# Feed-forward with seven block products: buffers for sums of weights, two products' weights made earlier, token sums in quarters

## The chip, the cores and the metric

The kernel runs on one core of a Trainium2 chip. The metric is the time on the device in microseconds (us) of one execution; the median of some runs is given. The five engines of the core are named as in the profile: PE (matmul; PEld is its weight load), DVE (VectorE), ACT (ScalarE), POOL (GpSimd) and SP (SyncE, which issues the transfers here).

## The reference, cut to what matters

The reference is two blocks of a transformer on 1024 tokens of width 1024. The change lies in the last part of the second block, the feed-forward with a gate: 5632 columns up (2816 of gate, 2816 of value), a causal convolution over three tokens for each column, and 2816 rows down.

```python
f = causal_dwconv(rms_norm_2(h, norm_ffn_pre[l]) @ ffn_up[l], ffn_conv[l])
gate, val = jnp.split(f, 2, axis=-1)
f = (jax.nn.gelu(gate, approximate=True) * val) @ ffn_down[l]
h = h + rms_norm_2(f, norm_ffn_post[l])
```

## The kernel before, in words

The program is written for a framework with tiles and pools: the author writes operations and buffers, and a scheduler sets the order of the instructions on each engine from its own costs. A tile with `bufs=n` under one tag turns through n buffers, and who writes a buffer again waits until its last reader is done.

Every fp32 operand of a matmul is held as two parts, high and low (`split`, lines 99 to 106: ACT rounds the high part, line 103, and DVE subtracts it, line 106). A product of two operands then takes three matmuls: high with high, high with low, low with high.

**Output projection** (`out_proj2`, to line 1617). It takes nine token tiles (t = -1 to 7). For each it multiplies by the output weights (128x512 matmuls, line 132 to 134), scales by the norm, adds the residual, writes the sum to HBM, norms again, transposes on PE (line 255) and leaves the columns in `hf` (line 1609). The two quadrants of `hf` that products use as they are go to `quads` as high and low parts (q0, q1).

**Up projection** (`ffn`, from line 1656). It runs 22 blocks j, and each makes 128 gate columns and 128 value columns of all tokens. Weights (two halves of the 1024 rows by gate and value columns) and tokens (two halves of the rows by two halves of the tokens) are each cut into 2x2 quadrants, and seven products instead of eight make the block (`SEVEN`): five of them take a sum or difference of two weight quadrants, and five take a sum or difference of two token quadrants.

- `up_raw` loads a block's weights as two transfers of 512 KB into `upraw` (two buffers).
- `up_op` makes the weights of product i in two pieces (128 x 2 x 128 each). Where a sum is wanted, POOL adds into `uptmp` (line 1648), ACT rounds it into `uph` and DVE makes `upl`. Before, `uptmp` has `bufs=1` in each of two pools, `w1` and `wp`, of which the pieces of line 1667 take `w1` nine times in eleven. The results `uph`, `upl` have two buffers in `wp` and nine in `w1`.
- `tok_op` makes the token sums s2 to s6 once, in block 0, and keeps them. Each sum is made in two slices of 4 x 258 or 4 x 256 columns: an add into the one buffer `tsum` (line 1682; POOL for i = 4 and 6, DVE for the rest), then a split.
- `block` runs the products. A product is two column ranges c of 12 matmuls of 128x258 each (lines 1700 to 1702), so a block is 7 x 2 x 12 = 168. ACT copies products 0 to 2 out of PSUM into `fs` (line 1706), DVE adds products 3 to 6 to them (`fx`, lines 1712 to 1720), POOL combines the `fs` (lines 1709, 1710, 1713, 1716), and `gate` makes the convolution and the gate: ACT (lines 1801, 1807), DVE (line 1803 eight times and line 1808 twice a block, both 128x512). Two transfers write `fd` to HBM (line 1809).

`ahead(t)` in `build` loads block 0's weights during the output projection and makes the weights of product 0.

**Down projection** (line 1780). It loads `fd` and the down weights and takes 22 steps for each half of the tokens; its first two steps are made ready during the up projection.

Of the kernel before, what the change touches and what calls it, by code (L numbers as in the profile page):

```python
# [13 lines left out]
F32 = mybir.dt.float32  # L14
F32R = mybir.dt.float32r
# [16 lines left out]
class Builder:  # L32
# [1601 lines left out]
            raws.append(raw)  # L1634
        return raws

    def up_op(self, raws, i, pools):

        nc = self.nc
        (r, h), sign, other = self.SEVEN[i][:3]  # L1640
        parts = []
        for raw in raws:
            pool, bufs = next(pools)
            src = raw[:, h, :, 128 * r:128 * r + 128]
            if sign:
                r2, h2 = other
                tmp = pool.tile([128, 2, 128], F32, tag="uptmp", name="uptmp", bufs=1)
                nc.gpsimd.tensor_tensor(tmp, src, raw[:, h2, :, 128 * r2:128 * r2 + 128],  # L1648
                                        op=ALU.add if sign > 0 else ALU.subtract)
                src = tmp  # L1650
            p = [pool.tile([128, 2, 128], F32R, tag="up" + z, name="up" + z, bufs=bufs) for z in "hl"]
            self.split(*p, src)
            parts.append(p)
        return lambda k: tuple(z[:, k % 2] for z in parts[k // 2])

    def ffn(self, hd, hf, close_hf, quads, wp, early, out):

        nc, I = self.nc, self.I
        st = ExitStack()
        sp = st.enter_context(self.pool("hS", 1))  # L1660
        w1 = st.enter_context(self.pool("wtsu", 1))
        p = st.enter_context(self.pool("ffn", 2))
# [1 line left out]
        nc.sync.dma_start(cw, I["ffn_conv"])  # L1664
        fd = [self.dp.tile([128, 2, 512], F32, name=f"fd{j}") for j in range(22)]
        self.psum(mm="ABDCABDE")
        pools = itertools.cycle([(wp, 2)] + [(w1, 9)] * 4 + [(wp, 2)] + [(w1, 9)] * 5)
        halves = [slice(0, 512), slice(512, 1024)]
        sums = {}

        def tok_op(i):

            qa, sign, qb = self.SEVEN[i][3:]
            if not sign:
                return quads[qa[0]]
            if i not in sums:
                a, b = (hf[:, 4 * r:4 * r + 4, 512 * h:512 * h + 514] for r, h in (qa, qb))
                op = [sp.tile([128, 4, 514], F32R, name=f"s{i}{z}") for z in "hl"]
                for c in (slice(0, 258), slice(258, 514)):
                    s = (slice(None), slice(None), c)  # L1680
                    t = sp.tile([128, 4, 258], F32, tag="tsum", name="tsum")[:, :, :c.stop - c.start]
                    (nc.gpsimd if i in (4, 6) else nc.vector).tensor_tensor(
                        t, a[s], b[s], op=ALU.add if sign > 0 else ALU.subtract)
                    self.split(op[0][s], op[1][s], t)
                sums[i] = op
            return sums[i]

        def block(j, raws, first):

            x = [[p.tile([128, 2, 258], F32, tag=f"fx{part}", name="fx") for part in range(2)] for c in range(2)]  # L1690
            s = [[None] * 7 for c in range(2)]
            for i in range(7):
                w = first if first and i == 0 else self.up_op(raws, i, pools)
                op = tok_op(i)
                for c in range(2):
                    ps = self.mm()[:, :258]
# [26 lines left out]
        raws, w0 = early  # L1723
# [17 lines left out]
        with ExitStack() as s2:  # L1741
            for j in range(22):
                if j:
                    raws, w0 = self.up_raw(j, wp), None
                block(j, raws, w0)
                if j == 0:
                    close_hf()
                    P = s2.enter_context(self.pool("dn1", 1, side="right"))
                if j == 20:
                    ready = [step(0, 0), step(0, 1)]  # L1750
# [60 lines left out]
    def build(self, out):  # L1811
# [77 lines left out]
        with ExitStack() as st:  # L1889
# [8 lines left out]
            def ahead(t):  # L1898
                if t == 3:
                    raws = self.up_raw(0, wp)  # L1900
                    early.extend((raws, self.up_op(raws, 0, itertools.repeat((wp, 2)))))

            self.out_proj2(wo2, oin2, o2, lod, hd, gp[:, 1], hf, quads, ahead)
            wos.close()
# [153 lines left out]
```

## Time and profile before

| | us |
|---|---|
| median of 3 runs | 3214.81 (3198.78 to 3215.32) |
| the profiled execution, its own time | 3207.53 |
| its span, first to last instruction | 3205.6 |
| PE busy over the span | 3034.4 (95%) |
| DVE, ACT, POOL busy | 1986.4 (62%), 1478.8 (46%), 786.2 (25%) |
| mean granted clock of TensorE | 0.972 |
| output projection 2 and first up products | about 2280 to 2404 |
| up projection, first matmul to last | 2391.2 to 2957.6 |
| down projection to the end | 2957.6 to 3205.6 |

Times in rows are counted from the start of the span. The median lies 7.3 us above the profiled execution's own time. The granted clock of a stretch is a share of full speed (2.4 GHz); 0.5 is the lower level, 1.2 GHz. Matmul durations overlap, so the distance between two starts is the time one takes of PE, and a stretch in which PE is "busy" throughout can still be slow at the lower clock.

### The profile page before, as it was taken

The page shows a single profiled execution, that of the slowest core. Times are in us where ns is not written, and L with a number is a line of the kernel's source. Part 1 is how long each engine was busy: PE and PEld are TensorE (multiplying, and loading weights), DVE is VectorE, ACT ScalarE, POOL GpSimd, SP SyncE. Part 2 cuts the span into 40 slices and gives each one's busy share as a digit, 9 for nine tenths or more (in the row PEclk, how much of TensorE's full clock was granted, in tenths as well). Part 3 has the DMA queues.
Part 4 walks back from the last instruction along what each step waited for, and adds up shares of the span by engine and source line. Part 5 has one row for each costly group of instructions (what it writes and reads, how often), then busy time and mean ns, then how long its engine had stood idle before and what let it go on. Part 6 is the DMA issues. An engine that isn't in the chain of part 4 may idle for free.

```text
span 3205.6 us, 54674 instructions
## 1 busy us (share of the span) xinstructions
PE 3034.4 (95%) x20419; PEld 2749.9 (86%) x20419; DVE 1986.4 (62%) x5238; ACT 1478.8 (46%) x3740; POOL 786.2 (25%) x892
## 2 busy tenths in 40 slices
PE   8899999999999999998999999999997999999999
PEld 5799999889877889997889898788877888888887
DVE  5667757777765755545457344766458677777453
ACT  4689845555653733332254222447434444444332
POOL 2466622332220000000000000110016565665000
PEclk9999999999999999999999999899997999999999
DMA  5222210010042221213311222313222122122552
GB/s 210 68 79 86 85 39 14 25 34 14 21 146 100 104 82 55 66 46 116 105 56 56 62 66 55 73 45 101 84 91 64 63 80 67 67 66 86 188 195 97
DMA packets 164137, 252.99 MB, mean 79 GB/s; under 512 B 25800, under 2 KB 93440, under 8 KB 163872
## 3 DMA queue, kind: packets, MB, share of 16 engines
q1 hardware_dynamic: 163872, 249.50, 24.3%
q8 instruction: 160, 2.62, 0.4%
q14 instruction: 105, 0.86, 0.1%
HBM read 194.94 MB, written 54.51 MB: 78 GB/s over the span
## 4 chain that ended last, share of the span: by engine, by line
PE 71%; DVE 12%; ACT 5%; POOL 5%; DMA 4%; issue 3%; SPq 0%; DVEq 0%; POOLq 0%; ACTq 0%
PE mm L132 12%; PE mm L133 12%; PE mm L134 12%; PE dn L1780 8%; DVE fy L1803 3%; PE te L405 3%; PE po L1534 3%; PE sc L391 3%; DVE upl L106 2%; PE po L661 2%; POOL uptmp L1648 2%; PE po L612 2%; PE mm L1702 1%; PE mm L1700 1%; PE mm L1701 1%
## 5 line engine op out<-in xcount | busy, mean ns | idle before, releaser
L132 PE MATMUL mm<-whi,hT 128*128 128x256 f32 (+1 forms) x1760 | 516.3, 294 | 17.5 <-DVE gs L428 4.7
L133 PE MATMUL mm<-wlo,hT 128*128 128x256 f32 (+1 forms) x1760 | 508.8, 289 | 1.9 <-POOL wlo L106 1.9
L132 PEld LDWEIGHTS mm<-whi,hT 128*128 128x128 f32 x1760 | 339.3, 193 | 25.1 <-DVE gs L428 5.0
L133 PEld LDWEIGHTS mm<-wlo,hT 128*128 128x128 f32 x1760 | 339.5, 193 | 5.3 <-POOL wlo L106 2.4
L97 POOL TENSOR_TENSOR inv<-inv,cm 128x1 f32<-128x1 f32 (+1 forms) x87 | 50.1, 576 | 1030.0 <-DVE inv L95 1029.9
L134 PE MATMUL mm<-whi,lo 128*128 128x256 f32 x1040 | 301.7, 291 | 0.9 <-POOL lo L106 0.8
L1648 POOL TENSOR_TENSOR uptmp<-upraw 128x256 f32<-128x256 f32 x220 | 199.2, 908 | 287.4 <-DVE upl L106 196.2
L97 POOL TENSOR_TENSOR c<-c,cm 128x2 f32<-128x2 f32 (+1 forms) x170 | 126.5, 745 | 402.3 <-DVE c L95 357.9
L132 PE MATMUL mm<-hT,whi 128*128 128x352 f32 (+3 forms) x640 | 219.2, 343 | 4.5 <-ACT a L1018 1.8
L133 PE MATMUL mm<-hT,whi 128*128 128x352 f32 (+3 forms) x640 | 217.7, 340 | 0.1
L134 PE MATMUL mm<-hT,wlo 128*128 128x352 f32 (+3 forms) x640 | 217.4, 341 | 0.0
L407 ACT COPY wT<-te 128x512 f32<-128x512 f32 (+2 forms) x368 | 159.1, 453 | 119.9 <-PE te L405 111.0
L134 PE MATMUL mm<-whi,hT 128*128 128x256 f32 (+3 forms) x720 | 206.3, 287 | 0.0
L134 PEld LDWEIGHTS mm<-whi,lo 128*128 128x128 f32 x1040 | 202.8, 195 | 3.4 <-POOL lo L106 1.8
L1803 DVE SCALAR_TENSOR_TENSOR fy<-fx,ffnc,fy 128x512 f32<-128x512 f32 x176 | 152.9, 895 | 11.3 <-ACT fy L1801 10.9
L103 ACT CAST uph<-uptmp 128x256 fp32r<-128x256 f32 x220 | 88.9, 405 | 152.2 <-POOL uptmp L1648 148.0
L106 DVE TENSOR_TENSOR upl<-uptmp,uph 128x256 fp32r<-128x256 f32 x220 | 110.6, 505 | 76.3 <-ACT uph L103 75.6
L397 DVE TENSOR_SCALAR_CACHE_REDUCE EB<-sc 128x512 f32<-128x512 f32 (+1 forms) x208 | 120.0, 584 | 35.9 <-PE sc L391 33.2
L182 POOL TENSOR_TENSOR adacc<-adacc,adpr 128x512 f32<-128x512 f32 (+1 forms) x112 | 129.0, 1152 | 47.9 <-ACT adpr L179 32.8
L103 ACT CAST whi<-wraw 128x512 fp32r<-128x512 f32 (+2 forms) x120 | 84.1, 719 | 118.4 <-PE mm L133 45.4
L391 PE MATMUL sc<-kT,qTh 128*128 128x256 f32 (+2 forms) x352 | 125.5, 371 | 13.3 <-DVE EB L397 6.6
L134 PEld LDWEIGHTS mm<-whi,hT 128*128 128x128 f32 (+1 forms) x720 | 136.5, 190 | 1.5
(543 smaller groups left out, 9208.9 us busy)
## 6 DMA issues: line engine op xcount, KB each, us to landing
adraw<-in_adaln_w SPq DMA_DIRECT2D x48, 512.0 KB, 3.8
upraw<-in_ffn_up SPq DMA_DIRECT2D x44, 512.0 KB, 3.7
dnraw<-in_ffn_down SPq DMA_DIRECT2D x88, 256.0 KB, 3.4
wraw<-in_w_ab SPq DMA_DIRECT2D x26, 512.0 KB, 3.7
woraw<-in_w_out SPq DMA_DIRECT2D x48, 256.0 KB, 2.8
wraw<-in_w_gla SPq DMA_DIRECT2D x48, 256.0 KB, 2.8
wraw<-in_w_in SPq DMA_DIRECT2D x24, 512.0 KB, 4.2
fd<-fy SPq DMA_DIRECT2D x44, 256.0 KB, 2.5
```

What stands on the lines that cost most here:

```text
L97: nc.gpsimd.tensor_tensor(out, out, self.cm05[:p, :n], op=ALU.pow)
L103: nc.scalar.copy(hi, src)
L106: (lo_eng or nc.vector).tensor_tensor(lo, src, hi.bitcast(F32), op=ALU.subtract)
L132: mmul(ps, ah, bh, start=k == 0, stop=False)
L133: mmul(ps, ah, bl, start=False, stop=False)
L134: mmul(ps, al, bh, start=False, stop=k == nk - 1)
L182: nc.gpsimd.tensor_tensor(a, a, pr[:, :conds], op=ALU.add)
L391: self.nc.tensor.matmul(sp, q[x][:, m], keys, start=x == 0, stop=last and x == 1)
L407: nc.scalar.copy(w[:n, :m, :nq], ps.rearrange("p (j t) -> p j t", j=4)[:n, :m, :nq])
L1648: nc.gpsimd.tensor_tensor(tmp, src, raw[:, h2, :, 128 * r2:128 * r2 + 128], op=ALU.add if sign > 0 else ALU.subtract)
L1780: nc.tensor.matmul(banks[t][i], a[e], b[g], start=k == 0 and n == 0, stop=k == 21 and n == 2)
L1803: nc.vector.scalar_tensor_tensor(y, x[part][:, :, tap:tap + 256], cw[:, tap, c:c + 1], y, op0=ALU.mult, op1=ALU.add)
```

## The change

`up_op` gets the pool and the number of buffers of `uptmp` as arguments. In `ffn` all sums of weights go through four buffers in `w1`; the results turn through seven buffers in `w1` and four in `wp`, eleven as before. During the output projection the weights of products 0 and 1 are made (before: 0), with one `uptmp` and four result buffers in `wp`, and `block` takes a list of ready products. A token sum is made in four quarters of 2 x 258 or 2 x 256 columns through a `tsum` of half the size, and the sum of i = 4 moves from POOL to DVE. No matmul is added or removed, and the transfers are the same.

```diff
--- before.py
+++ after.py
@@ -1634,21 +1634,21 @@
             raws.append(raw)
         return raws
 
-    def up_op(self, raws, i, pools):
+    def up_op(self, raws, i, pools, tp, bufs):
 
         nc = self.nc
         (r, h), sign, other = self.SEVEN[i][:3]
         parts = []
         for raw in raws:
-            pool, bufs = next(pools)
+            pool, n = next(pools)
             src = raw[:, h, :, 128 * r:128 * r + 128]
             if sign:
                 r2, h2 = other
-                tmp = pool.tile([128, 2, 128], F32, tag="uptmp", name="uptmp", bufs=1)
+                tmp = tp.tile([128, 2, 128], F32, tag="uptmp", name="uptmp", bufs=bufs)
                 nc.gpsimd.tensor_tensor(tmp, src, raw[:, h2, :, 128 * r2:128 * r2 + 128],
                                         op=ALU.add if sign > 0 else ALU.subtract)
                 src = tmp
-            p = [pool.tile([128, 2, 128], F32R, tag="up" + z, name="up" + z, bufs=bufs) for z in "hl"]
+            p = [pool.tile([128, 2, 128], F32R, tag="up" + z, name="up" + z, bufs=n) for z in "hl"]
             self.split(*p, src)
             parts.append(p)
         return lambda k: tuple(z[:, k % 2] for z in parts[k // 2])
@@ -1664,7 +1664,7 @@
         nc.sync.dma_start(cw, I["ffn_conv"])
         fd = [self.dp.tile([128, 2, 512], F32, name=f"fd{j}") for j in range(22)]
         self.psum(mm="ABDCABDE")
-        pools = itertools.cycle([(wp, 2)] + [(w1, 9)] * 4 + [(wp, 2)] + [(w1, 9)] * 5)
+        pools = itertools.cycle([(w1, 7)] * 7 + [(wp, 4)] * 4)
         halves = [slice(0, 512), slice(512, 1024)]
         sums = {}
 
@@ -1676,10 +1676,11 @@
             if i not in sums:
                 a, b = (hf[:, 4 * r:4 * r + 4, 512 * h:512 * h + 514] for r, h in (qa, qb))
                 op = [sp.tile([128, 4, 514], F32R, name=f"s{i}{z}") for z in "hl"]
-                for c in (slice(0, 258), slice(258, 514)):
-                    s = (slice(None), slice(None), c)
-                    t = sp.tile([128, 4, 258], F32, tag="tsum", name="tsum")[:, :, :c.stop - c.start]
-                    (nc.gpsimd if i in (4, 6) else nc.vector).tensor_tensor(
+                for z in range(4):
+                    c = slice(0, 258) if z < 2 else slice(258, 514)
+                    s = (slice(None), slice(z % 2 * 2, z % 2 * 2 + 2), c)
+                    t = sp.tile([128, 2, 258], F32, tag="tsum", name="tsum")[:, :, :c.stop - c.start]
+                    (nc.gpsimd if i == 6 else nc.vector).tensor_tensor(
                         t, a[s], b[s], op=ALU.add if sign > 0 else ALU.subtract)
                     self.split(op[0][s], op[1][s], t)
                 sums[i] = op
@@ -1690,7 +1691,7 @@
             x = [[p.tile([128, 2, 258], F32, tag=f"fx{part}", name="fx") for part in range(2)] for c in range(2)]
             s = [[None] * 7 for c in range(2)]
             for i in range(7):
-                w = first if first and i == 0 else self.up_op(raws, i, pools)
+                w = first[i] if i < len(first) else self.up_op(raws, i, pools, w1, 4)
                 op = tok_op(i)
                 for c in range(2):
                     ps = self.mm()[:, :258]
@@ -1741,7 +1742,7 @@
         with ExitStack() as s2:
             for j in range(22):
                 if j:
-                    raws, w0 = self.up_raw(j, wp), None
+                    raws, w0 = self.up_raw(j, wp), []
                 block(j, raws, w0)
                 if j == 0:
                     close_hf()
@@ -1898,7 +1899,7 @@
             def ahead(t):
                 if t == 3:
                     raws = self.up_raw(0, wp)
-                    early.extend((raws, self.up_op(raws, 0, itertools.repeat((wp, 2)))))
+                    early.extend((raws, [self.up_op(raws, i, itertools.repeat((wp, 4)), wp, 1) for i in range(2)]))
 
             self.out_proj2(wo2, oin2, o2, lod, hd, gp[:, 1], hf, quads, ahead)
             wos.close()
```

On POOL, in the middle of the up projection, a block's ten `uptmp` adds and eight `fs` operations stood like this before (one block and the start of the next):

```order
L1648 TENSOR_TENSOR uptmp<-upraw 128x256 x5
L1709 TENSOR_TENSOR fs_31199<-fs_31199,fs_31115 128x258
L1648 TENSOR_TENSOR uptmp<-upraw 128x256
L1709 TENSOR_TENSOR fs_31216<-fs_31216,fs_31130 128x258
L1710 TENSOR_TENSOR fs_31199<-fs_31199,fs_31157 128x258
L1710 TENSOR_TENSOR fs_31216<-fs_31216,fs_31172 128x258
L1648 TENSOR_TENSOR uptmp<-upraw 128x256
L1713 TENSOR_TENSOR fs_31115<-fs_31199,fx 128x258
L1713 TENSOR_TENSOR fs_31130<-fs_31216,fx 128x258
L1648 TENSOR_TENSOR uptmp<-upraw 128x256
```

and stand like this now (the lines are one higher, so 1710 here is 1709 before):

```order
L1648 TENSOR_TENSOR uptmp<-upraw 128x256 x4
L1710 TENSOR_TENSOR fs_30923<-fs_30923,fs_30839 128x258
L1648 TENSOR_TENSOR uptmp<-upraw 128x256 x2
L1710 TENSOR_TENSOR fs_30940<-fs_30940,fs_30854 128x258
L1711 TENSOR_TENSOR fs_30923<-fs_30923,fs_30881 128x258
L1648 TENSOR_TENSOR uptmp<-upraw 128x256
L1711 TENSOR_TENSOR fs_30940<-fs_30940,fs_30896 128x258
L1648 TENSOR_TENSOR uptmp<-upraw 128x256
L1714 TENSOR_TENSOR fs_30839<-fs_30923,fx 128x258
L1648 TENSOR_TENSOR uptmp<-upraw 128x256
L1717 TENSOR_TENSOR fs_30881<-fs_30923,fx 128x258
L1714 TENSOR_TENSOR fs_30854<-fs_30940,fx 128x258
```

The adds stood in runs of five and more with the `fs` operations together; now one or two adds alternate with them, and this pattern repeats from block to block.

On DVE, in block 0, after `hf` is complete, the token sums s3 and s4 stood like this before (`upl` is the low part of weights, `fx` a product added up):

```order
L1682 TENSOR_TENSOR tsum<-hf 128x1032
L106 TENSOR_TENSOR upl<-uptmp,uph 128x256 x2
L106 TENSOR_TENSOR upl<-upraw,uph 128x256 x3
L106 TENSOR_TENSOR s3l<-tsum,s3h 128x4x258
L106 TENSOR_TENSOR upl<-uptmp,uph 128x256
L1682 TENSOR_TENSOR tsum<-hf 128x4x256
L1712 TENSOR_TENSOR fx<-mm,fs_27585 128x258
L106 TENSOR_TENSOR s3l<-tsum,s3h 128x4x256
L106 TENSOR_TENSOR upl<-uptmp,uph 128x256
L1712 TENSOR_TENSOR fx<-mm,fs_27600 128x258
L106 TENSOR_TENSOR s4l<-tsum,s4h 128x4x258
```

and stand like this now:

```order
L1683 TENSOR_TENSOR tsum<-hf 128x516
L106 TENSOR_TENSOR upl<-uptmp,uph 128x256
L106 TENSOR_TENSOR s3l<-tsum,s3h 128x2x258
L1683 TENSOR_TENSOR tsum<-hf 128x516
L106 TENSOR_TENSOR s3l<-tsum,s3h 128x2x258
L1683 TENSOR_TENSOR tsum<-hf 128x2x256
L106 TENSOR_TENSOR s3l<-tsum,s3h 128x2x256
L1713 TENSOR_TENSOR fx<-mm,fs_27597 128x258
L1683 TENSOR_TENSOR tsum<-hf 128x2x256
L106 TENSOR_TENSOR s3l<-tsum,s3h 128x2x256
L106 TENSOR_TENSOR upl<-uptmp,uph 128x256
L1683 TENSOR_TENSOR tsum<-hf 128x516
```

Each sum is now four adds and four low parts, the adds of s4 stand on DVE too, and less other work stands between an add and its low part.

## Rows read from the trace of the kernel before

**Rows 1.** Windows over the core: stretch, length, busy time (instructions) of each engine, clock, DMA.
```profile
2280.00:2300.00 20.00, 19.81 (x97) 12.40 (x97) 6.66 (x15) 4.98 (x13) 3.29 (x5) 1.00 0.44 135
2384.00:2445.00 61.00, 42.56 (x221) 37.24 (x219) 43.08 (x54) 21.63 (x43) 32.48 (x28) 0.73 0.10 36
2445.00:2957.00 512.00, 463.68 (x3517) 443.89 (x3518) 372.27 (x678) 233.44 (x552) 308.99 (x373) 0.96 0.22 71
2823.00:2833.00 10.00, 10.00 (x86) 10.00 (x85) 4.29 (x10) 3.47 (x11) 7.91 (x12) 1.00 0.31 103
2600.00:2603.00 3.00, 2.92 (x14) 2.62 (x14) 2.90 (x5) 2.14 (x6) 1.36 (x2) 0.50 0.00 0
```

**Rows 2.** Waits from 2445 to 2957 us: who waited for whom, us, times, longest.
```profile
POOL uptmp L1648 <- DVE upl L106: 180.7, 120, 3.8
...
PEld mm L1702 <- DVE upl L106: 39.6, 41, 2.4
...
PEld mm L1700 <- ACT uph L103: 27.8, 49, 1.3
...
POOL uptmp L1648 <- DMA upraw<-in_ffn_up: 5.2, 9, 2.5
```

**Rows 3.** Timeline, the rows of one weight sum (start, us, instruction [idle before]).
```profile
2602.20 0.73 POOL L1648 TENSOR_TENSOR uptmp<-upraw 128x256 f32<-128x256 f32 x1 [1.57 <-DVE upl L106]
...
2602.96 0.41 ACT L103 CAST uph<-uptmp 128x256 fp32r<-128x256 f32 x1 [0.77 <-POOL uptmp L1648]
...
2603.40 0.43 DVE L106 TENSOR_TENSOR upl<-uptmp,uph 128x256 fp32r<-128x256 f32 x1
...
2603.90 0.74 POOL L1648 TENSOR_TENSOR uptmp<-upraw 128x256 f32<-128x256 f32 x1 [0.98 <-DVE upl L106]
```

**Rows 4.** By tile, the repeated operations: duration ns min/median/max, first and last start.
```profile
L1648 POOL TENSOR_TENSOR uptmp<-upraw x220: 721/749/1773, 2289.5 to 2948.4; 128x256 f32<-128x256 f32 x110
L106 DVE TENSOR_TENSOR upl<-uptmp,uph x220: 406/422/2620, 2290.8 to 2949.6; 128x256 fp32r<-128x256 f32 x110
L1803 DVE SCALAR_TENSOR_TENSOR fy<-fx,ffnc,fy x176: 734/744/1686, 2442.9 to 2960.9; 128x512 f32<-128x512 f32 x176
L1710 POOL TENSOR_TENSOR fs<-fs,fs x44: 725/759/1712, 2417.7 to 2950.7; 128x258 f32<-128x258 f32 x44
L1712 DVE TENSOR_TENSOR fx<-mm,fs x44: 412/427/429, 2417.1 to 2950.1; 128x258 f32<-128x258 f32 x44
```

**Rows 5.** Timelines of DVE and POOL: instructions back to back, merged.
```profile
2620.67 0.75 DVE L106 TENSOR_TENSOR upl<-uptmp,uph 128x256 fp32r<-128x256 f32 x2
2643.81 1.40 DVE L1803 SCALAR_TENSOR_TENSOR fy<-fx,ffnc,fy 128x512 f32<-128x512 f32 x2
2637.50 1.43 POOL L1648 TENSOR_TENSOR uptmp<-upraw 128x256 f32<-128x256 f32 x2
```

**Rows 6.** Timelines of POOL and DVE at 2447 us, beside each other.
```profile
2446.97 2.85 POOL L1682 TENSOR_TENSOR tsum<-hf 128x1024 f32<-128x1024 f32 x1 [1.77 <-DVE s6l L106]
2447.48 2.62 DVE L106 TENSOR_TENSOR upl<-uptmp,uph 128x256 fp32r<-128x256 f32 x1
```

**Rows 7.** By tile, the token sums, with their last ACT and DVE parts.
```profile
L1682 DVE TENSOR_TENSOR tsum<-hf x6: 1220/1224/1761, 2391.8 to 2437.5; 128x1032 f32<-128x1032 f32 x3, 128x1024 f32<-128x1024 f32 x3
L1682 POOL TENSOR_TENSOR tsum<-hf x4: 2365/2536/2846, 2421.0 to 2447.0; 128x1032 f32<-128x1032 f32 x2, 128x1024 f32<-128x1024 f32 x2
L103 ACT CAST s6h<-tsum x2: 1052/1052/1053, 2444.1 to 2449.9; 128x1032 fp32r<-128x1032 f32 x1, 128x1024 fp32r<-128x1024 f32 x1
L106 DVE TENSOR_TENSOR s6l<-tsum,s6h x2: 1211/1215/1219, 2445.7 to 2453.3; 128x1032 fp32r<-128x1032 f32 x1, 128x1024 fp32r<-128x1024 f32 x1
```

**Rows 8.** Timelines of PE and DVE: a wait for product 1's weights, the last `hf`.
```profile
2397.60 0.39 PE L1702 MATMUL mm<-q1h,upl 128*128 128x258 f32 x1 [2.59 <-DVE upl L106]
...
2404.20 0.69 DVE L1609 TENSOR_TENSOR hf<-tp,gp 128x512 f32<-128x512 f32 x1 [1.21 <-PE tp L255]
```

## The prediction

> **What bounds the kernel now.** The change lies in the up projection, so I read its stretch alone, first the windows, then the waits, then one weight sum in order of time. From 2445 to 2957 us [rows 1] PE runs 3517 matmuls of 128x258. A block has 168, so these are 3517 / 168 = 20.93 blocks of 512 / 20.93 = 24.46 us. What PE needs at full speed is seen in the ten-microsecond window at clock 1.00 [rows 1]: 86 matmuls, about two of which only overlap its edges, so 84 in 10 us or 0.119 us each, and 168 x 0.119 = 20.0 us a block. The loss is 4.46 us a block, 93 us in all. It has two parts. PE's weight loads wait 39.6 us for `upl` and 27.8 us for `uph` [rows 2], together 67.4. Most of the rest is the clock: it is 0.96 in the mean [rows 1], and in the 3 us window behind such a wait it is at the lower of its two levels, 0.50 (1.2 GHz). With 8% of 512 us at half speed that is 41 us in which some 20 are lost.
>
> Why are weights late? POOL waits 180.7 us for `upl` in the same stretch [rows 2], 8.6 us a block; it is busy for 308.99 / 20.93 = 14.8 us [rows 1]. Together 23.4 of 24.46: POOL's queue has almost no other time, so the chain through POOL paces the block. One round of it stands in rows 3: an add at 2602.20, ACT's `uph`, DVE's `upl`, and the next add only at 2603.90, when `upl` has freed the one `uptmp`: 1.70 us for an add that takes 0.70 back to back [rows 5]. In POOL's queue the `fs` operations stand behind the adds, so they can't fill these waits.
>
> **The change, part by part.**
>
> *Four buffers for weight sums.* An add now needs the `upl` of four adds earlier to be done, and the `fs` operations stand between single adds. POOL's waits of 8.6 us a block are what goes. Next in line are, per block: PE with 20.0 us; POOL with 18 operations x 0.70 [rows 4, 5] = 12.6 us of its own; DVE with 14 `upl` x 0.34, 8 `fx` taken at the same 0.34 (both take 0.41 to 0.43 [rows 4]) and ten operations of 128x512 x 0.66 [rows 4, 5], 4.8 + 2.7 + 6.6 = 14.1 us; ACT with 233.44 / 20.93 = 11.2 us [rows 1]. So PE is next, if POOL and DVE don't hinder each other.
>
> They do. DVE is busy for 372.27 / 20.93 = 17.8 us instead of 14.1, POOL 14.8 instead of 12.6. In rows 6 a POOL add of 2.85 us runs and an `upl`, 0.41 us alone, takes 2.62: it waits for the add's end. The trace does not show what this costs once POOL no longer pauses, so I bound it. If the two take turns, and each holds the other off only while it passes columns, a POOL add holds (2365 - 721) / (1032 - 256) = 2.12 ns a column [rows 4, 7], 0.54 us for 256, and DVE (1220 - 406) / 776 = 1.05 ns, 0.27 us for an `upl` and 0.54 for 512 columns. `fx` reads one side from PSUM and I leave it out. Then 18 x 0.54 + 14 x 0.27 + 10 x 0.54 = 18.9 us a block, below PE's 20.0. If each holds the other off for the time it takes in its queue, it is 12.6 + 14 x 0.34 + 10 x 0.66 = 24.0 us. Rows 6 are near the first: the wait of 2.62 - 0.41 = 2.2 us is 1024 columns x 2.12 ns. 18.9 of 20.0 is dense, and both queues run in order, so I take **20.9 us a block**: PE's 20.0 and 0.9 of late weights. Gain: 20.93 x (24.46 - 20.9) = **74.5 us**; the ends are 93 (20.0) and 10 (24.0).
>
> The Trainium skill has a rule against this change ("SBUF — State Buffer", section "SBUF: two separate sides"): a DVE operation with two SBUF inputs and a GpSimd operation that reads SBUF take an exclusive lock, held for the full instruction, and the other one fully blocks. Read literally it gives the 24.0 us and a gain of 10 us; the trace agrees that the other blocks, and rows 6 put what is held nearer to the columns than to the instruction.
>
> *Loads.* On SP a block's two loads and two `fd` writes stand in the same order as before. POOL waits for loads 5.2 us in all, 2.5 at the longest [rows 2]; were it 2.5 in every block, POOL would have 14.8 + 2.5 = 17.3 us, still under PE. Cost 0. The eleven result buffers are as many as before.
>
> *Product 1's weights in the output projection.* Two adds, two `uph` and two `upl` more at about 2290, with one `uptmp`, so two rounds of 1.70 us. There DVE is busy 6.66 of 20 us, ACT 4.98 and POOL 3.29, while PE has 19.81 [rows 1]: cost 0, and 3.4 us if POOL's small norm operations behind them were late for PE. Late in the projection, the wait of 2.59 us for these weights [rows 8] goes.
>
> *Token sums in quarters.* From the last `hf` (2404.9) to the last part of s6 (2453.3 + 1.2) block 0 takes 49.6 us [rows 7, 8], and PE is busy for 42.56 of 61 us there at clock 0.73 [rows 1]. One `tsum` makes the slices follow one another. Before: a slice on DVE is 1.22 + 1.05 + 1.22 = 3.5 us, one on POOL 2.37 + 1.05 + 1.22 = 4.6; five and four of them after `hf` are 36 us, and the other 14 are queueing. Now: a quarter has 516 columns, 0.68 us on DVE and 1.27 on POOL by the slopes above, ACT some 0.62 (between 0.41 and 1.05 [rows 3, 7]); 14 quarters x 1.98 and 4 on POOL x 2.57 are 38 us. So quarters alone lengthen the chain by 2 us; two POOL adds of 2.4 that held DVE off go away, and the weights' own chain no longer stands between. PE can start a product on a first quarter 1.5 us sooner. I take a gain of **3 us** with the 2.6 of product 1, between a loss of 5 and a gain of 12 (most of the queueing).
>
> *Down projection.* Its first loads stand in the up projection as before, its other work is untouched: 0.
>
> Sum: 3207.5 (own time of the profiled execution) - 74.5 - 3 = **3130 us**. The median of the runs shown is 7.3 us above that execution, within their scatter of 16.
>
> **The rivals.**
>
> *POOL and DVE take turns by whole instructions.* 24.0 us a block: 3207.5 - 10 - 3 = 3195 us. For it: `upl` at 2.62 us [rows 6]. Against it: 17.8 + 14.8 us busy in a block of 24.46 overlap by over 8 us, waits included, and the slopes.
>
> *DVE becomes the bound through its order.* `fx` waits for PE, `fy` for ACT, `upl` for all three; its busy time grows with the density (3.7 us of waiting x 24.46 / 20 = 4.5, so 18.6), and idle time of 4 us (now 24.46 - 17.8 = 6.7) gives 22.6: 3207.5 - 39 - 3 = 3166 us.
>
> *Slower: POOL, no longer waiting, holds DVE off each time.* Place: DVE's queue in each block. Each of POOL's 18 operations costs DVE 0.54 us: 14.1 + 9.7 = 23.8. From 0.7 us of other idle time on, a block is longer than now; with half of today's idle time (3.3) it is 27.1: 3207.5 + 20.93 x 2.6 - 3 = 3259 us. Against it: eight `fx` of a block need no turn, and DVE would then run behind PE, which takes most of its idle time away.
>
> *The change doesn't do what it says.* `upl` stays late because the eleven result buffers, not `uptmp`, hold the adds back: 3205 us. Against it: the add at 2603.90 comes right behind `upl` [rows 3], as 120 do [rows 2].
>
> **How the numbers follow.** Forecast (blocks of 20.0 to 22.2 us) 0.76; DVE the bound 0.10; turns by whole instructions 0.07; slower 0.04; no effect 0.03. The range takes in the first two: from 3207.5 - 93 - 12 = 3102, and 2 for the runs' scatter, so 3100, up to DVE's 3166 and 10 for scatter, 3176. About 0.5% (16 us) is what a measurement of this kernel can tell from no change. Faster by more than that 0.86 (the first two cases), within it 0.10 (whole turns, no effect), slower 0.04.
>
> **What would show it.** In the changed profile POOL's waits for `upl` should fall from 180.7 us to under 40, PE's waits for `upl` and `uph` from 67 to under 20, the clock of the stretch rise from 0.96 to 0.99 or more, blocks come every 20 to 22 us, and `uptmp` and `fy` have longer means than before. Block 0 should take about as long. I am wrong if blocks stay above 23 us, if DVE is busy over 95% of the stretch while PE waits, or if the time comes from elsewhere than blocks 1 to 21.

## The result, and the profile after

| | before | after |
|---|---|---|
| median of 4 runs, us | 3208.73 (3198.78 to 3215.32) | 3167.87 (3163.32 to 3171.09) |
| ratio after / before | | 0.9874, 95% interval 0.984 to 0.9908 |
| profiled execution, own time | 3207.53 | 3171.09 |
| span | 3205.6 | 3169.3 |
| last `hf` to first `fx` of product 6 (block 0) | 48.7 | 50.3 |
| first to last `fx` of product 6 (21 blocks) | 505.0 | 465.2 |
| from there to the end of the span | 247.7 | 244.5 |

The median before is 3208.73 with a fourth run, where three gave 3214.81. The kernel is faster by 1.3%. The forecast was 3130 us, its range 3100 to 3176. The time lies in the range, but only because the range was drawn to take in the rival in which DVE becomes the bound through its order (3166 us); about half of the forecast gain came.

The last three rows of the table place the gain. They come from starts of `hf` [rows 8] and of `fx` of product 6, whose rows by tile are, before and after:

```profile
L1720 DVE TENSOR_TENSOR fx<-mm,fs x44: 411/414/427, 2452.9 to 2957.9; 128x258 f32<-128x258 f32 x44
```

```profile
L1609 DVE TENSOR_TENSOR hf<-tp,gp x18: 167/684/692, 2308.9 to 2409.3; 128x512 f32<-128x512 f32 x16, 128x8 f32<-128x8 f32 x2
L1721 DVE TENSOR_TENSOR fx<-mm,fs x44: 411/414/428, 2459.6 to 2924.8; 128x258 f32<-128x258 f32 x44
```

The 21 blocks are 39.8 us shorter. Block 0 is 1.6 us longer, and what follows 3.2 us shorter. Everything up to the last `hf`, where the code is the same but for product 1's weights, took 5.1 us longer in this execution (in the other profiled executions of this study the last `hf` starts anywhere from 2395.9 to 2409.4, so this lies within their scatter). Together -39.8 + 1.6 - 3.2 + 5.1 = -36.3, the difference of the spans.

Of the 21 blocks after, those from the fourth to the twentieth take 22.39 to 22.48 us each; the mean is 22.15 because the last one, behind which no weights are made, takes 16.5.

The windows of the kernel after, with the columns of [rows 1]; the last one is exactly one block. Below them stands the third window of the kernel before, for comparison:

```profile
2384.00:2445.00 61.00, 46.04 (x224) 38.90 (x223) 47.29 (x75) 23.52 (x54) 26.61 (x28) 0.79 0.11 36
2445.00:2922.00 477.00, 438.07 (x3553) 428.76 (x3552) 409.21 (x679) 221.38 (x551) 325.35 (x372) 1.00 0.23 76
2540.00:2640.00 100.00, 91.10 (x742) 89.15 (x741) 83.35 (x143) 44.22 (x112) 70.19 (x83) 1.00 0.22 73
2568.38:2590.78 22.40, 20.62 (x170) 20.23 (x168) 19.07 (x32) 10.23 (x26) 15.47 (x19) 1.00 0.22 71
```

```profile
2540.00:2640.00 100.00, 89.46 (x682) 85.47 (x681) 70.58 (x131) 44.53 (x107) 61.33 (x77) 0.97 0.23 74
```

The clock of the stretch is 1.00 where it was 0.96. DVE, whose busy time is the third in a row, was busy for 70.58 of the 100 us from 2540 in the kernel before and is now busy for 83.35. The waits from 2445 to 2922 us, which answer to [rows 2]:

```profile
POOL uptmp L1648 <- DVE upl L106: 126.9, 52, 9.1
...
DVE fx L1719 <- POOL fs L1717: 62.2, 19, 3.7
...
PE mm L1701 <- DVE fx L1719: 32.7, 37, 1.4
...
PEld mm L1701 <- DVE fx L1719: 28.8, 20, 1.6
...
POOL uptmp L1648 <- DMA upraw<-in_ffn_up: 11.2, 5, 3.6
```

The 67.4 us for which PE's weight loads waited for `upl` and `uph` [rows 2] are gone but for 2.2. What PE now waits for is `fx` of product 5 (line 1719): DVE's read of a PSUM bank that the next product needs. Its weight loads wait 28.8 us for it and its matmuls 32.7; the two overlap and can't be added. That `fx` in turn waits 62.2 us for POOL's `fs` of line 1717, which makes s1 ready for it. One block in order of time, the rows that bear on it (first of POOL and DVE, then of PE):

```profile
2564.43 0.62 DVE L106 TENSOR_TENSOR upl<-upraw,uph 128x256 fp32r<-128x256 f32 x1
...
2567.71 0.64 POOL L1717 TENSOR_TENSOR fs<-fs,fx 128x258 f32<-128x258 f32 x1
2568.38 0.43 DVE L1719 TENSOR_TENSOR fx<-mm,fs 128x258 f32<-128x258 f32 x1 [3.33 <-POOL fs L1717]
...
2574.99 1.18 POOL L1648 TENSOR_TENSOR uptmp<-upraw 128x256 f32<-128x256 f32 x1 [4.29 <-DVE upl L106]
2577.86 1.94 POOL L1648 TENSOR_TENSOR uptmp<-upraw 128x256 f32<-128x256 f32 x2 [1.68 <-DVE upl L106]
2580.27 0.75 DVE L106 TENSOR_TENSOR upl<-uptmp,uph 128x256 fp32r<-128x256 f32 x2
2580.76 0.86 POOL L1648 TENSOR_TENSOR uptmp<-upraw 128x256 f32<-128x256 f32 x1 [0.96 <-DVE upl L106]
...
2590.11 0.64 POOL L1717 TENSOR_TENSOR fs<-fs,fx 128x258 f32<-128x258 f32 x1
2590.78 0.43 DVE L1719 TENSOR_TENSOR fx<-mm,fs 128x258 f32<-128x258 f32 x1 [3.33 <-POOL fs L1717]
```

```profile
2568.95 0.36 PE L1701 MATMUL mm<-s2h,uph 128*128 128x258 f32 x1 [0.44 <-DVE fx L1719]
```

This is a closed loop of 22.40 us. From 2568.38 DVE works without a pause through the gate's operations and the `upl` between them. Meanwhile POOL stands at four adds (2574.99, two from 2577.86, and 2580.76) that are in a row in its queue, ahead of the block's first `fs`; each needs a buffer that an `upl` in DVE's stretch frees, the last one that of 2580.27. (The remark ahead of the prediction that one or two adds alternate with the `fs` holds only behind these four.) From 2580.76 POOL works without a pause through adds and `fs` in its order, and only at 2590.11 comes the `fs` for which DVE waits. DVE's 19.07 us of work and this one wait of 3.33 fill the block, 22.40; so do POOL's 15.47 and its three waits of 4.29, 1.68 and 0.96. The wait of 3.33 us comes back, within 0.01, in every block from 2545.98 to 2904.55.

The order alone would not make the loop longer than PE's 20.0 us; this is an estimate from rows. DVE's stretch, from 2568.38 to 2580.76, takes 12.4 us for 20 operations (four `fx`, seven `upl`, eight `fy` and a gate's product), which by the times of one alone [rows 4, 5] need 11 x 0.34 + 9 x 0.66 = 9.7. POOL's stretch, from there to the end of its `fs` at 2590.75, takes 10.0 for 12 operations, which alone need 12 x 0.70 = 8.4. Without the 4.3 us by which the two engines lengthen each other there, the loop would take some 18.1. So the loop is longer than PE's work through both together, the order and the lengthening.

The operations by tile, as in [rows 4]:

```profile
L1648 POOL TENSOR_TENSOR uptmp<-upraw x220: 726/916/1241, 2294.7 to 2905.2; 128x256 f32<-128x256 f32 x110
L106 DVE TENSOR_TENSOR upl<-uptmp,uph x220: 403/617/1185, 2295.9 to 2914.9; 128x256 fp32r<-128x256 f32 x110
L1804 DVE SCALAR_TENSOR_TENSOR fy<-fx,ffnc,fy x176: 734/741/1795, 2448.1 to 2927.8; 128x512 f32<-128x512 f32 x176
L1719 DVE TENSOR_TENSOR fx<-mm,fs x44: 408/416/426, 2446.9 to 2922.8; 128x258 f32<-128x258 f32 x44
```

### The profile page after: what moved, and what is told of

Same layout as the page of the kernel before. It is cut to its first block, busy times and chain, and to the rows that moved or that the text cites. A ratio compares the mean times of both kernels' runs of the same rounds, so it can differ in the third digit from the quotient of the medians.

```text
span 3169.3 us, 55151 instructions
## 1 busy us (share of the span) xinstructions
PE 3016.6 (95%) x20419; PEld 2741.6 (87%) x20419; DVE 2027.5 (64%) x5258; ACT 1468.2 (46%) x3750; POOL 797.2 (25%) x892
## 5 line engine op out<-in xcount | busy, mean ns | idle before, releaser
L1781 PE MATMUL dn<-dnl,fh 128*128 128x512 f32 x352 | 137.3, 390 | 0.0
L1781 PE MATMUL dn<-dnh,fl 128*128 128x512 f32 x352 | 137.3, 391 | 0.0
```

The source lines that it names most:

```text
L1781: nc.tensor.matmul(banks[t][i], a[e], b[g], start=k == 0 and n == 0, stop=k == 21 and n == 2)
```

## The experiments

Twelve kernels were run, each beside the kernel before, whose median in these groups was 3205.3 to 3208.6 us; medians of different groups therefore compare to some 3 us. The block below is the distance from the first to the last `fx` of product 6 over 21 (up to 0.15 us too long, since it ends with a second column range). DVE's shares are its busy time, and its waits for POOL, ACT or PE, in the 100 us from 2540.

| kernel | median, us | ratio to before (95%) | block, us | DVE busy | DVE waits |
|---|---|---|---|---|---|
| before | 3208.73 | | 24.05 | 70.6 | 29.1 |
| after | 3167.87 | 0.9874 (0.984 to 0.9908) | 22.15 | 83.4 | 16.7 |
| e1_evac | 3161.31 | 0.9853 (0.9829 to 0.9877) | 21.71 | 89.6 | 10.4 |
| e2_dve | 3147.93 | 0.9819 (0.98 to 0.9839) | 21.36 | 95.3 | 4.7 |
| e3_one | 3245.86 | 1.0123 (1.0104 to 1.0142) | 26.14 | 65.6 | 33.5 |
| e4_four | 3165.73 | 0.988 (0.9855 to 0.9905) | 21.86 | 83.7 | 17.6 |
| e5_pre | 3151.99 | 0.9828 (0.9813 to 0.9844) | 21.27 | 89.5 | 11.6 |
| e6_pre_dve | 3158.05 | 0.9844 (0.9828 to 0.9861) | 21.60 | 95.9 | 4.0 |
| e7_pre_mul | 3149.93 | 0.9822 (0.9804 to 0.984) | 21.50 | 92.3 | 7.7 |
| e8_nomul | 3149.44 | 0.9816 (0.9794 to 0.9838) | 21.25 | 77.7 | 22.1 |
| e9_six | 3172.89 | 0.9891 (0.9873 to 0.9909) | 22.71 | 78.1 | 24.1 |
| e10_dve_six | 3182.26 | 0.9919 (0.9899 to 0.9939) | 23.08 | 77.8 | 22.3 |
| e11_pre_six | 3171.96 | 0.9882 (0.9861 to 0.9903) | 22.36 | 77.9 | 22.1 |
| e12_pre_raw3 | 3145.61 | 0.9816 (0.9796 to 0.9835) | 21.45 | 91.9 | 8.1 |

### e1_evac

```diff
-                        nc.gpsimd.tensor_tensor(s0, s2, u[:, 0], op=ALU.add)
-                        nc.gpsimd.tensor_tensor(s1, s2, g[:, 1], op=ALU.add)
-                        nc.vector.tensor_tensor(u[:, 1], ps, s1, op=ALU.add)
+                        nc.vector.tensor_tensor(u[:, 1], ps, s2, op=ALU.add)
+                        nc.gpsimd.tensor_tensor(u[:, 1], u[:, 1], g[:, 1], op=ALU.add)
-                        nc.vector.tensor_tensor(g[:, 0], ps, s0, op=ALU.add)
+                        nc.vector.tensor_tensor(g[:, 0], ps, s2, op=ALU.add)
+                        nc.gpsimd.tensor_tensor(g[:, 0], g[:, 0], u[:, 0], op=ALU.add)
```

> The changed kernel, in which DVE's adds for products 5 and 6 take s2 straight from `fs2` and POOL adds the other summand afterwards (u1 += g1, g0 += u0), in place of POOL's updates of s0 and s1 ahead of them. Counts and sizes of operations on POOL and DVE are the same; sums are rounded in another order. Theory A (a PSUM bank is freed late, since DVE's `fx` of product 5 waits for POOL's `fs` in POOL's in-order queue, which makes a loop of 22.40 us a block): PE no longer waits for `fx`, DVE no longer waits for POOL's `fs` behind product 4, blocks 20.3 to 21.0 us, 3125 to 3140 us. Rival B (POOL's and DVE's operations are dense and lengthen one another, whatever their order): as many operations, so blocks stay at 22.2 to 22.6 us and the time at 3163 to 3172 us.

The wait of DVE for POOL's `fs` is gone as theory A has it, but the time fell by 7 us, a fifth of what theory A gives, and the interval overlaps that of the changed kernel; it lies in neither range. A new wait came two steps later: ACT's first step of the gate waits for POOL's additions to `fx` (91.2 and 39.6 us from 2445 to 2922, about as long as for DVE's `fx` in the changed kernel, 102.6 and 32.0), and DVE's second step now waits for ACT, 2.1 us a block. DVE's busy time rose from 83.4 to 89.6 of 100 us with as many operations. Theory A named a right wait, but what it costs is not what a block loses.

### e2_dve

```diff
-                        nc.gpsimd.tensor_tensor(s1, s2, g[:, 1], op=ALU.add)
+                        nc.vector.tensor_tensor(s1, s2, g[:, 1], op=ALU.add)
```

> The changed kernel with one POOL operation of each column range moved to DVE: the update of s1 behind product 4 (s2 + g1), for which DVE's `fx` of product 5 waits. Theory A: the 3.3 us a block for which DVE waits for it go, blocks 20.5 to 21.5 us, 3130 to 3150 us. Rival B (density): POOL has 2 operations a block less and DVE 2 more, some 0.3 to 0.7 us each way, so blocks stay within 0.7 us of 22.4 and the time between 3153 and 3183 us.

Inside A's range, and 20 us below the changed kernel; the two intervals don't meet. The windows and DVE's waits from 2470 to 2900 us:

```profile
2470.00:2900.00 430.00, 417.98 (x3338) 405.18 (x3337) 403.74 (x686) 204.76 (x516) 289.66 (x310) 1.00 0.23 80
```

```profile
DVE fy L1804 <- ACT fy L1802: 15.1, 19, 0.8
DVE fs L1717 <- POOL fs L1711: 8.6, 19, 1.7
```

DVE is now busy for 403.74 of 430 us and has almost no waits left, and still a block takes 21.36 us where PE needs 20.0. With the wait cut, DVE's queue is all but full: 20.1 us a block, of which 14.8 are its operations alone (14.1 and two more of 0.34) and the rest is lengthening. That DVE's work is then the bound is read from this and not shown by a run of its own.

### e3_one and e4_four

```diff
-                w = first[i] if i < len(first) else self.up_op(raws, i, pools, w1, 4)
+                w = first[i] if i < len(first) else self.up_op(raws, i, pools, w1, 1)
```

> The changed kernel with one buffer for sums of weights in the up projection in place of four; product 1's early weights, the token sums in quarters and the ring of results stay. If the four buffers are what made blocks 22.4 in place of 24.46 us: back to 24.2 to 24.8 us a block and 3205 to 3218 us. If the new ring of results (7 and 4 buffers) or the other two parts brought it: 22.4 to 23 us a block and 3165 to 3180 us.

```diff
-                tmp = pool.tile([128, 2, 128], F32, tag="uptmp", name="uptmp", bufs=1)
+                tmp = tp.tile([128, 2, 128], F32, tag="uptmp", name="uptmp", bufs=n4)
-        pools = itertools.cycle([(wp, 2)] + [(w1, 9)] * 4 + [(wp, 2)] + [(w1, 9)] * 5)
+        pools = itertools.cycle([(wp, 2)] + [(w1, 8)] * 4 + [(wp, 2)] + [(w1, 8)] * 4)
-                w = first if first and i == 0 else self.up_op(raws, i, pools)
+                w = first if first and i == 0 else self.up_op(raws, i, pools, w1, 4)
```

> The kernel before with four buffers for sums of weights and nothing else of the change, but for the ring of results, which has ten buffers in place of eleven so that all fits. If the blocks carry the whole gain: 22.3 to 22.6 us a block and 3163 to 3175 us, and block 0 ends about where it did before. If quarters and early weights carry a part of it, 3175 to 3195 us. If ten results are too few, PE waits for `uph` and `upl` and the time is above 3195 us.

(The diff of e4_four leaves out the lines that only pass the new arguments on.) Four buffers alone (with ten results in place of eleven), without the quarters and without product 1's early weights, give 3165.73 us: the whole of the gain, as expected. Its blocks are shorter than expected, 21.86 us, and its block 0 is longer than before, 52.5 us against 48.7. The other parts together can't be told from nothing. Everything but the four buffers (e3_one) is 1.2% slower than the kernel before, 26.14 us a block; it was expected at 3205 to 3218 us. Its waits from 2470 to 2900 us show the weights late again, for ACT's part and for DVE's:

```profile
POOL uptmp L1648 <- DVE upl L106: 181.5, 118, 3.3
...
PEld mm L1701 <- ACT uph L103: 43.3, 64, 2.2
...
PEld mm L1703 <- DVE upl L106: 38.3, 39, 1.9
```

Before, a block had its sums turn through two buffers, one in each pool; here all turn through one. I take that for the reason, but it wasn't tried alone.

### e5_pre, e6_pre_dve and e7_pre_mul

```diff
-                        nc.scalar.copy(s[c][i], ps)
-                    if i == 2:
-                        nc.gpsimd.tensor_tensor(s2, s2, s0, op=ALU.subtract)
-                        nc.gpsimd.tensor_tensor(s2, s2, s1, op=ALU.subtract)
+                    if i < 2:
+                        nc.scalar.copy(s[c][i], ps)
+                    elif i == 2:
+                        nc.gpsimd.tensor_tensor(s2, s0, s1, op=ALU.add)
+                        nc.vector.tensor_tensor(s2, ps, s2, op=ALU.subtract)
```

> The changed kernel with s2 made in another way: POOL adds fs0 + fs1 already after product 1, and DVE takes s2 = product 2 minus that sum straight from PSUM. POOL has 16 operations a block instead of 18, ACT two copies less, DVE two operations more (0.34 us each, one side from PSUM). Theory C (after the first runs: DVE's in-order queue is the bound; in the changed kernel it is busy for 19.1 of 22.40 us a block, 14.1 of its own and 5.0 lengthened by POOL, and the other 3.3 it waits for POOL's `fs` behind product 4): two POOL operations of 0.9 us less stand ahead of that `fs`, so the wait falls from 3.3 to about 1.5 us, DVE's busy time stays at 19.1 to 19.4, blocks 20.5 to 21.2 us, 3125 to 3143 us. Rival D (POOL's `fs` is late because weight adds ahead of it wait for `upl`, which a shorter chain of `fs` doesn't change): the wait stays over 2.5 us, blocks 21.9 to 22.4 us, 3155 to 3168 us.

In its DVE waits from 2470 to 2900 us the wait for POOL is halved (27.6 us, where the changed kernel has 55.2 in the same window), to some 1.4 us a block, as theory C has it:

```profile
DVE fx L1720 <- POOL fs L1718: 27.6, 19, 1.9
DVE fy L1805 <- ACT fy L1803: 13.8, 18, 0.8
```

The time fell by 16 us, less than the 25 to 43 expected: a new wait for ACT of 0.8 us a block stands in DVE's queue, and PE now waits for the bank that DVE's new operation on product 2 frees (line 1712, 15.5 us in its matmuls and 22.8 in its weight loads).

e6_pre_dve is e5_pre with the edit of e2_dve.

> The edit of e5_pre together with that of e2_dve (the update of s1 behind product 4 on DVE). POOL has 14 operations a block, DVE four more than in the changed kernel. Theory C: DVE 15.5 us of its own and 5.0 x 14 / 18 = 3.9 from POOL, 19.4, and under 1 us of waiting: blocks 20.2 to 20.9 us, where PE's 20.0 is almost the bound; 3118 to 3137 us. Rival D (what counts is the number of DVE operations with both sides in SBUF, so that the shift to DVE costs what it saves): 21.2 to 21.6 us a block as in e2_dve, 3141 to 3152 us.

The two edits that gain 20 and 16 us alone gain 10 together, outside both ranges. DVE's waits are down to 4.0 of 100 us, but its busy time is at 95.9: four operations more than in the changed kernel, two of them with both sides in SBUF (up to 0.96 us each beside POOL).

e7_pre_mul is e5_pre with one operation moved from DVE to POOL:

```diff
-        nc.vector.tensor_tensor(g, g, u, op=ALU.mult)
+        nc.gpsimd.tensor_tensor(g, g, u, op=ALU.mult)
```

> The edit of e5_pre, and the product of gate and value (128x512, twice a block) on POOL instead of DVE. Theory C: DVE 14.8 - 1.3 = 13.5 us of its own and 5 to 5.5 from POOL, so 18.5 to 19; POOL 16 operations of 0.9 and two of 1.4 to 2, so 17.5 to 18.5 us, and the `fs` behind product 4 comes later where such an operation stands ahead of it: 20.2 to 21.5 us a block, 3118 to 3150 us. Rival E (POOL is as near to the bound as DVE): over 21.5 us a block and 3150 to 3175 us, slower than e5_pre.

3149.93 us is not to be told from e5_pre, and it lies where the two ranges meet, so it decides between neither. DVE lost two operations of 128x512 a block and is busy for more of the time than there, 92.3 against 89.5 us of 100, while POOL is busy for 78.3 against 64.5. I read this as POOL lengthening the rest of DVE's operations (the median of `upl<-upraw` goes from 417 to 610 ns); it was not tried apart.

### e8_nomul

```diff
-        nc.vector.tensor_tensor(g, g, u, op=ALU.mult)
```

> The changed kernel without the product of gate and value: two DVE operations of 128x512 a block are left out (1.22 us each in its profile). Theory C (DVE's queue sets the pace, with its wait for POOL): the block shortens by what they take, 1.3 to 2.4 us, to 20.0 to 21.1 us; 3118 to 3141 us. Theory A alone (the loop runs over POOL's queue and PSUM, and DVE's busy time does not matter): blocks stay at 22.2 to 22.4 us, 3163 to 3168 us.

Two DVE operations of 1.22 us left out shorten the block by 0.90 us, and DVE's waits rise from 16.7 to 22.1 of 100 us. That fits the loop as the rows show it: in the changed kernel one of the two (2579.13 us) stands in DVE's stretch before POOL is let go, and the other (2580.94) behind it, where DVE waits for POOL anyway. The time, 18 us below the changed kernel, lies between the two ranges: neither "DVE's sum" (1.3 to 2.4 us a block) nor "not DVE at all" (0) is right.

### e9_six, e10_dve_six and e11_pre_six

```diff
-                w = first[i] if i < len(first) else self.up_op(raws, i, pools, w1, 4)
+                w = first[i] if i < len(first) else self.up_op(raws, i, pools, w1, 6)
-        pools = itertools.cycle([(w1, 7)] * 7 + [(wp, 4)] * 4)
+        pools = itertools.cycle([(w1, 6)] * 6 + [(wp, 4)] * 4)
```

> The changed kernel with six buffers for sums of weights (and ten results, as in e4_four, so that it fits). Theory G (after eight runs: the period of 22.40 us in the changed kernel is one loop over two in-order queues: DVE's stretch from `fx` of product 5 over the gate's operations to the `upl` that lets POOL go on, 12.3 us, and POOL's stretch of adds and `fs` without a pause up to the `fs` that this `fx` waits for, 9.4 us, with some 0.7 us of handing over): two more adds run while DVE is in its stretch, so POOL's has two of 0.88 us less, blocks some 1.8 us shorter by rows, 20.4 to 21.2 us, 3128 to 3150 us, and POOL waits for `upl` some 4 us a block less. Rival C (DVE's busy time with its one wait is the bound, whatever POOL has ready): DVE's wait stays, 22 to 22.4 us, 3160 to 3168 us. If ten results are too few, PE waits for `uph` or `upl`, and it is slower than 3168 us.

e10_dve_six has the edit of e2_dve as well, e11_pre_six that of e5_pre.

> The edits of e2_dve and e9_six together: six buffers, and the update of s1 behind product 4 on DVE. In e2_dve DVE is busy for 95% of the stretch, and its only waits are short. Theory G (loop): with the loop already cut, two more buffers take nothing more than POOL's short waits; 3140 to 3150 us, as e2_dve. Rival H (DVE's operations, lengthened by POOL's, are then the bound, and POOL's adds in other places lengthen others of them): anything within 3135 to 3165 us with DVE busy over 94%.

> The edits of e5_pre and e9_six together. e5_pre left DVE waiting 1.9 us a block for POOL's `fs` and 0.8 us for ACT's `fy`. Theory G (loop): six buffers take away most of the 1.9 us, blocks some 1 to 1.9 us shorter than in e5_pre, 3113 to 3133 us. Rival H (DVE's busy time rises as its wait falls): 3140 to 3155 us, as e5_pre.

All three missed: six buffers bring nothing to the changed kernel and cost 34 and 20 us in the other two. POOL's waits from 2470 to 2900 us, in e9_six:

```profile
POOL uptmp L1648 <- DMA upraw<-in_ffn_up: 103.6, 24, 7.4
```

POOL no longer waits for `upl` (3.7 us) but for the loads, 103.6 us where the changed kernel has 10.4 in this window. The two `upraw` hold one block; DVE's last `upl` from them lets the next load start, and that takes 4.2 us (median). With six buffers the scheduler also set other orders (in e9_six POOL's `fs` stand in a row at the end), the clock is back to 0.97, and DVE waits more. Waits for loads alone need not cost time: e2_dve, one of the fastest, has 91.6 us of them in this window. Which of the two costs the time here, the loads or the order, stays open.

### e12_pre_raw3

```diff
-            raw = pool.tile([128, 2, 2, 256], F32, tag="upraw", name="upraw", bufs=2)
+            raw = pool.tile([128, 2, 2, 256], F32, tag="upraw", name="upraw", bufs=3)
-        pools = itertools.cycle([(w1, 7)] * 7 + [(wp, 4)] * 4)
+        pools = itertools.cycle([(w1, 7)] * 7 + [(wp, 2)] * 2)
-                    early.extend((raws, [self.up_op(raws, i, itertools.repeat((wp, 4)), wp, 1) for i in range(2)]))
+                    early.extend((raws, [self.up_op(raws, i, itertools.repeat((wp, 2)), wp, 1) for i in range(1)]))
```

> The kernel of e5_pre with three buffers for loaded weights (`upraw`) in place of two. To make room, there are nine results in place of eleven and only product 0's weights are made in the output projection. POOL's order in a block stays that of e5_pre. Theory L (after eleven runs: with two `upraw`, which is one block, the loop closes over the load: DVE's `upl<-upraw`, which stands behind the `fx` that waits for POOL's `fs`, frees the buffer, then the load takes 3.5 us, and only then POOL's adds of the next block start, and its `fs`): POOL's waits for loads fall from 104 us in the stretch to under 40, DVE's wait for POOL's `fs` from 27.6 to under 12, blocks from 21.3 to 20.2 to 20.9 us, 3127 to 3146 us. Rival H (DVE's operations, lengthened by POOL's, fill the time that the wait leaves): POOL's waits for loads fall as well, but DVE is busy over 93% and the time stays at 3146 to 3160 us. If nine results are too few, PE waits for `uph` or `upl` over 30 us and it is slower than that.

The waits for loads are gone from its list altogether, and the time is 0.2% below e5_pre, within both intervals. POOL's waits from 2470 to 2900 us, and DVE's:

```profile
POOL fs L1711 <- ACT fs L1709: 83.5, 21, 5.9
...
POOL uptmp L1648 <- DVE upl L106: 57.3, 78, 1.3
```

```profile
DVE fx L1720 <- POOL fs L1718: 24.2, 20, 1.5
```

POOL's pause of some 4 us a block now ends with ACT's copy of product 1, and DVE's wait stays. The time lies in theory L's range, but its signs did not come: DVE's wait was to fall under 12 us, and blocks to 20.9 or less; they take 21.45. So theory L, by which the load closes the loop, is not borne out. That the load was one of several waits that would have ended at nearly the same moment fits this, but was not tried.

Of the versions that compute everything, e12_pre_raw3 (3145.61 us) and e2_dve (3147.93) are the fastest and can't be told apart, nor clearly from e7_pre_mul (3149.93); e2_dve is one word away from the changed kernel.

## Why the prediction was right, and where it was off

- **What bounded before**: right. One `uptmp` paced the block through POOL. With four buffers and little else the gain is all there (e4_four), with one it is gone (e3_one).
- **The direction and the range**: right; 40.9 us were gained by the medians, 77.5 forecast.
- **The steady block** is the step that failed: "So PE is next, if POOL and DVE don't hinder each other", and behind it the 20.9 us. Both of its checks, DVE's and POOL's busy time below PE's 20.0 us, compared sums. But both queues run in order and each waits for the other: POOL for DVE's `upl`, DVE for POOL's `fs`. The loop through the two takes 22.40 us, though neither is busy for more than 19.07 in it. Over 21 blocks 39.8 us were gained in place of 74.5. Some 8 us of the difference come from the base: 24.46 us a block was worked out from a count of matmuls in which records are missing (a window from 2452.9 to 2957.9 us has 3469 in the 21 blocks, which run 21 x 168 = 3528). By `fx` the mean is 24.05, and from there 20.9 us a block would have gained 66.
- **The rival "DVE becomes the bound through its order"** had the sum right, nearly by the parts: 18.6 us busy and 4 idle, 22.6; measured 19.07 and 3.33, 22.40. That is partly luck: its idle time of 4 us came from no row, just as the forecast's "0.9 of late weights" came from none, and its `fx` waits for PE, where the measured one waits for POOL. What the prediction didn't see is which wait would make DVE's idle time, though the order of POOL after the change, with four adds in a row and then an add or two before most `fs`, was there to be walked through.
- **Turns of POOL and DVE**: that they hold each other off by columns and not by whole instructions is near what was measured (last section). [Rows 6], on which the prediction rested this, don't decide it: the `upl` ends at 2450.10, 0.28 us behind the add's end at 2449.82, which whole instructions would give as well. The lengthening is in the loop with some 4.3 us. The Trainium skill has the lock held for the full instruction ("SBUF — State Buffer", section "SBUF: two separate sides"). Read so, a block would take 24.0 us by the prediction's working; the trace doesn't bear that out, with 22.40.
- **Slower, or no effect**: neither came. POOL waits less for `upl`, and PE no longer for weights.
- **Block 0**: a gain of 3 us was taken, between -5 and +12; from the last `hf` it is 1.6 us longer. PE's wait of 2.59 us for product 1's `upl` [rows 8] is gone, but it stood ahead of the last `hf`, where PE waits for the output projection's `xs` in either kernel (2.82 us before, 3.25 after). By the profiled executions it is not the quarters that lengthen block 0 but the four buffers, for which the prediction had no term there: 47.9 us with quarters and one buffer (e3_one), 52.5 with four buffers and whole slices (e4_four), 50.3 with both. Why was not looked for.
- **Loads**: cost 0 held, POOL waits 11.2 us for them in all. They are near, though: with a block shorter at another place they come to the front (e9_six).
- **Down projection**: 0 was taken; it is 3.2 us shorter in the profiled execution, and within 1.3 us of that in all twelve other kernels (244.5 to 245.8 us). Why was not looked for.
- **The signs**: the clock (1.00) and block 0 came as told. POOL's waits for `upl` fell to 126.9, not under 40; the 67.4 us of PE's weight loads for weights went, but 28.8 for a PSUM bank came in their place; blocks are just above 20 to 22. Longer means came only weakly: `uptmp` 908 to 932 ns (its median 749 to 916) and `fy` 895 to 900. It was `upl<-uptmp` that grew, from 505 to 600, and the gate's product, from 759 to 1156.

What stays open: why none of twelve kernels has a block under 21.2 us, when PE needs 20.0 and DVE's wait for POOL could be cut. In the 100 us from 2540 of each kernel with four buffers DVE is either busy or waits for POOL or ACT, never for PE; e2_dve and e6_pre_dve show that its work alone can fill 95% of the time. A kernel that takes work off DVE without giving it to POOL was tried only by leaving work out.

## What to carry to other kernels

When a buffer is added to break a chain of waits, don't compare the engines' busy sums only; look for the next loop that closes through two in-order queues, and add its stretches in the order that the new program has, with the operations as long as they are when both engines run. An operation that frees a PSUM bank should not wait for an engine whose queue is full of early work: moving that one small addition to the engine that frees the bank was worth nearly half as much as the whole change (20 of 40.9 us). And a wait that is taken away alone may be worth nothing where several end at the same moment.

## What the runs showed of the hardware

A POOL add and a DVE `upl` that stand side by side go on in step. From 2562.96 to 2564.74 of the changed kernel POOL starts an operation each 0.89 us and DVE an `upl` and an `fx` in the same 0.89:

```profile
2562.96 0.93 POOL L1711 TENSOR_TENSOR fs<-fs,fs 128x258 f32<-128x258 f32 x1
2563.85 0.91 POOL L1648 TENSOR_TENSOR uptmp<-upraw 128x256 f32<-128x256 f32 x1
2564.74 0.92 POOL L1711 TENSOR_TENSOR fs<-fs,fs 128x258 f32<-128x258 f32 x1
```

```profile
2562.66 0.63 DVE L106 TENSOR_TENSOR upl<-uptmp,uph 128x256 fp32r<-128x256 f32 x1
2563.21 0.41 DVE L1716 TENSOR_TENSOR fx<-mm,fs 128x258 f32<-128x258 f32 x1
2563.55 0.62 DVE L106 TENSOR_TENSOR upl<-uptmp,uph 128x256 fp32r<-128x256 f32 x1
```

Alone, POOL's takes 0.70 us and the `upl` 0.34 [rows 4, 5], together 1.04; by the slopes of the prediction 0.54 + 0.27 = 0.81. The measured 0.89 lies between, nearer to the slopes: here each holds the other off for less than its own turn in the queue. The `fx`, which reads one side from PSUM, was not lengthened once: 408 to 428 ns in all 176 of the changed kernel, while `upl<-uptmp` reaches 1185.
